# Layer normalisation without affine parts: an in-place ring of 8-row tiles, fixed engine orders and a short tail in place of six input and six output buffers of 4 rows

## The chip, the cores and the metric

The kernel runs on one core of one Trainium2 chip. The metric is the device time in microseconds (us) of a whole execution, the median of several; profiles give the span of one of them, which is about 2 us less. The kernel before takes 321.2 us. A run is called slow only when it is over 1.5% above the fastest of its kernel.

## The reference

```python
batch, seq, dim = 32, 512, 1024           # x: 16384 rows of 1024 float32, 67.1 MB
mean = np.mean(x, axis=-1, keepdims=True)
var = np.var(x, axis=-1, keepdims=True)
return ((x - mean) / np.sqrt(var + eps)).astype(np.float32)
```

Each row is read once and written once: 134.2 MB in all. Nothing can be left out.

## The kernel before

A tile is 4 rows a partition on 128 partitions, 2 MiB; a partition's 4 rows lie together in memory, so a DMA moves 128 pieces of 16 KiB, 8 on each of the 16 DMA engines. Loads are issued on the SyncE queue (q1 in the profile), stores on the ScalarE queue (q10).

```python
xin = ctx.enter_context(tc.tile_pool(name="xin", bufs=6))
yout = ctx.enter_context(tc.tile_pool(name="yout", bufs=6))
for t in range(ntiles):                                   # 32 tiles, K = 4
    xt = xin.tile([P, K, D], fdt)
    nc.sync.dma_start(out=xt, in_=x2[rows].rearrange("(p k) d -> p k d", p=P))
    ...      # VectorE: 2 bn_stats and 1 bn_aggr a row, then three tiny operations a tile
    ...      # ScalarE: square root; GpSimd: -mean * rstd
    yt = yout.tile([P, K, D], fdt)
    for k in range(K):
        nc.scalar.activation(out=yt[:, k, :], in_=xt[:, k, :], func=AF.Identity,
                             bias=nmr[:, k : k + 1], scale=rstd[:, k : k + 1])
    nc.scalar.dma_start(out=dst, in_=yt)
```

## Time and profile before

| | before |
|---|---|
| median time, us | 321.2 |
| span of the profiled run, us | 319.0 |
| busy: VectorE, ScalarE | 57%, 48% |
| DMA, mean of 16 engines | 98.8% of the span |
| rate between 40 and 280 us | 431 GB/s |
| last store's 16 landings: median, last | 315.69, 318.21 us |

The page is read from the DMA row: it is full from the second slice on, so engine times matter only where they empty a DMA queue. A DMA is complete when each of the 16 engines has reported; the trace holds those 16 reports. The difference between the last and the median one is called **lateness** below: 2.5 us before.

### The profile page before, as it was taken

To read this page: it belongs to the slowest core of one execution; us is meant where nothing else is said; L and a number is where in the kernel's file an instruction comes from. 1 tells how busy PE (TensorE), PEld (TensorE's weight loads), DVE (VectorE), ACT (ScalarE), POOL (GpSimd) and SP (SyncE) were. 2 spreads that over 40 slices of the span, in tenths; PEclk is the share of its full clock that TensorE was granted. 3 is DMA by queue.
4 is the path that set the end of the run, shared out by engine and by line. 5 is a ranking of instruction groups with operands and counts; after the bars stand their busy time and mean duration, and the time that the engine had idled before them with its cause. 6 is when DMAs were issued, how large, how long until landed. Compare 5 with 4: busy or idle time off the path is not lost.

```text
span 319.0 us, 926 instructions
## 1 busy us (share of the span) xinstructions
DVE 181.6 (57%) x480; ACT 154.3 (48%) x161; POOL 6.6 (2%) x36
## 2 busy tenths in 40 slices
DVE  0999764457754477544676355765446744467610
ACT  1147491651907419074380833809247091470970
POOL 0000000000000000000000000000000000000000
DMA  7999999999999999999999999999999999999995
GB/s 294 427 405 422 438 431 431 431 429 431 426 429 432 435 431 431 429 427 431 431 433 435 430 431 427 427 431 427 435 438 430 428 431 427 431 427 427 421 427 220
DMA packets 9222, 134.27 MB, mean 421 GB/s; under 512 B 1024, under 2 KB 1024, under 8 KB 1024
## 3 DMA queue, kind: packets, MB, share of 16 engines
q1 hardware_dynamic: 4608, 67.11, 49.6%
q10 hardware_dynamic: 4608, 67.11, 49.2%
q14 instruction: 6, 0.05, 0.0%
HBM read 67.11 MB, written 67.11 MB: 421 GB/s over the span
## 4 chain that ended last, share of the span: by engine, by line
DMA 87%; DVE 4%; issue 3%; ACT 2%; SPq 1%; POOLq 0%; POOL 0%; DVEq 0%
DMA xt<-in_x_dram 87%; DVE stats L53 3%; ACT yt L75 1%; SPq L47 1%; DVE mv L57 0%; DVE ivar L65 0%; DVE negmean L59 0%; POOLq L115 0%; ACT rstd L68 0%; POOL nmr L71 0%; DVE vpe L61 0%; DVEq L65 0%; DVEq L59 0%
## 5 line engine op out<-in xcount | busy, mean ns | idle before, releaser
L53 DVE BATCH_NORM_STATS2 stats<-xt 128x6 f32<-128x512 f32 x256 | 159.4, 665 | 115.3 <-DMA xt<-in_x_dram 115.3
L75 ACT ACTIVATE yt<-xt,nmr,rstd 128x1024 f32<-128x1024 f32 x128 | 146.7, 1227 | 4.7 <-POOL nmr L71 4.5
L68 ACT ACTIVATE rstd<-ivar 128x4 f32<-128x4 f32 x32 | 6.6, 205 | 149.6 <-DVE ivar L65 149.0
L57 DVE BATCH_NORM_AGGREGATE mv<-stats 128x2 f32<-128x12 f32 x128 | 25.1, 196 | 1.1
L71 POOL TENSOR_TENSOR nmr<-negmean,rstd 128x4 f32<-128x4 f32 x32 | 6.3, 198 | 297.9 <-ACT rstd L68 297.9
L65 DVE RECIPROCAL ivar<-vpe 128x4 f32<-128x4 f32 x32 | 5.7, 178 | 3.0
L59 DVE TENSOR_SCALAR negmean<-mv 128x4 f32<-128x4 f32 x32 | 5.4, 170 | 3.1
L61 DVE TENSOR_SCALAR vpe<-mv 128x4 f32<-128x4 f32 x32 | 5.2, 162 | 0.0
L68 ACT ACT_TABLE_LOAD x1 | 1.3, 1283 | 0.7 <-PEq L101 0.7
L101 POOL MEMSET const-float32-0.0<- 128x1 f32 x1 | 0.1, 98 | 0.2 <-issue 0.2
L101 POOL MEMSET const-uint8-127<- 128x1 uint8 x1 | 0.1, 102 | 0.0
L101 POOL MEMSET const-bfloat16-1.0<- 128x1 bf16 x1 | 0.1, 101 | 0.0
L101 POOL MEMSET const-float32-1.0<- 128x1 f32 x1 | 0.1, 98 | 0.0
## 6 DMA issues: line engine op xcount, KB each, us to landing
xt<-in_x_dram SPq DMA_DIRECT2D x32, 2048.0 KB, 38.4
out_dram<-yt ACTq DMA_DIRECT2D x32, 2048.0 KB, 15.5
```

The costliest lines, as they stand in the source:

```text
L47: nc.sync.dma_start(out=xt, in_=x2[rows].rearrange("(p k) d -> p k d", p=P))
L53: nc.vector.bn_stats(out=stats[:, k, s, :], in_=xt[:, k, s * BN_MAX : (s + 1) * BN_MAX],)
L57: nc.vector.bn_aggr(out=mv[:, k, :], in_=stats[:, k, :, :])
L59: nc.vector.tensor_scalar_mul(out=negmean, in0=mv[:, :, 0], scalar1=-1.0)
L61: nc.vector.tensor_scalar(out=vpe, in0=mv[:, :, 1], scalar1=eps_val, scalar2=None, op0=ALU.add)
L65: nc.vector.reciprocal(out=ivar, in_=vpe)
L68: nc.scalar.activation(out=rstd, in_=ivar, func=AF.Sqrt, bias=0.0, scale=1.0)
L71: nc.gpsimd.tensor_mul(out=nmr, in0=negmean, in1=rstd)
L75: nc.scalar.activation(out=yt[:, k, :], in_=xt[:, k, :], func=AF.Identity, bias=nmr[:, k : k + 1], scale=rstd[:, k : k + 1],)
L101: nc = _bacc.Bacc("TRN2", target_bir_lowering=False, num_devices=1)
```

## The change

The intent is to halve the number of packets (32 KiB instead of 16 KiB each), to write the result over the input so that all 192 KiB a partition serve both, to fix the order of instructions on each engine, to need fewer tiny operations, and to end on a small tile so that the last store is small and early. GROUP is the number of rows whose statistics are taken together; STORE is the number of rows after which a store is issued (16 is more than a tile, so there is one store a tile).

```diff
+TILES = (8, 8, 8, 8, 8, 8, 8, 8, 8, 8, 8, 8, 8, 8, 8, 6, 2)
+RING = 48
+GROUP = 4
+STORE = 16
-    xin = ctx.enter_context(tc.tile_pool(name="xin", bufs=6))
-    yout = ctx.enter_context(tc.tile_pool(name="yout", bufs=6))
+    ring = ring_pool.tile([P, RING, D], fdt)
...
-        nc.vector.tensor_scalar_mul(...)   # and add eps, reciprocal, ScalarE sqrt, GpSimd multiply
+        nc.scalar.activation(out=std[:, :G], in_=mv[:, :G, 1], func=AF.Sqrt, bias=eps_t, scale=1.0)
+        nc.vector.reciprocal(out=rstd[:, :G], in_=std[:, :G])
+        nc.vector.scalar_tensor_tensor(out=nmr[:, :G], in0=mv[:, :G, 0], scalar=-1.0,
+                                       in1=rstd[:, :G], op0=ALU.mult, op1=ALU.mult)
         for k in range(G):
             nc.scalar.activation(
-                out=yt[:, k, :],
+                out=xt[:, k, :],
...
+    with tc.manual_schedule():
+        nc.vector.memset(eps_t, eps_val)
+        for t, (K, row, pos) in enumerate(plan):
+            load(t)
+            ...                              # group(...) for every 4 rows, then store(...) for the tile
```

A load into a slot of the ring must now wait until the slot's store has landed.

More of the change, by code (lines that the diff above doesn't have):

```diff
@@ L26 @@
     BN_MAX = nc.vector.BN_STATS_FMAX
-    assert D % BN_MAX == 0
     NSUB = D // BN_MAX
-    K = 4
-    rows_per_tile = P * K
-    assert N % rows_per_tile == 0
-    ntiles = N // rows_per_tile
-    xin = ctx.enter_context(tc.tile_pool(name="xin", bufs=6))
-    yout = ctx.enter_context(tc.tile_pool(name="yout", bufs=6))
+    assert sum(TILES) * P == N
+    ring_pool = ctx.enter_context(tc.tile_pool(name="ring", bufs=1))
     st = ctx.enter_context(tc.tile_pool(name="st", bufs=4))
+    const = ctx.enter_context(tc.tile_pool(name="const", bufs=1))
     fdt = mybir.dt.float32
@@ L41, with load, group @@
     ALU = mybir.AluOpType
-    for t in range(ntiles):
-        rows = slice(t * rows_per_tile, (t + 1) * rows_per_tile)
-        xt = xin.tile([P, K, D], fdt)
-        nc.sync.dma_start(out=xt, in_=x2[rows].rearrange("(p k) d -> p k d", p=P))
-        stats = st.tile([P, K, NSUB, 6], fdt)
-        mv = st.tile([P, K, 2], fdt)
-        for k in range(K):
+    ring = ring_pool.tile([P, RING, D], fdt)
+    eps_t = const.tile([P, 1], fdt)
+    def load(t):
+        K, row, pos = plan[t]
+        rows = slice(row * P, (row + K) * P)
+        nc.sync.dma_start(
+            out=ring[:, pos : pos + K, :],
+            in_=x2[rows].rearrange("(p k) d -> p k d", p=P),
+        )
+    def group(xt, G):
+        stats = st.tile([P, GROUP, NSUB, 6], fdt, name="stats")
+        mv = st.tile([P, GROUP, 2], fdt, name="mv")
+        for k in range(G):
             for s in range(NSUB):
@@ L57 @@
             nc.vector.bn_aggr(out=mv[:, k, :], in_=stats[:, k, :, :])
-        negmean = st.tile([P, K], fdt)
-        nc.vector.tensor_scalar_mul(out=negmean, in0=mv[:, :, 0], scalar1=-1.0)
-        vpe = st.tile([P, K], fdt)
-        nc.vector.tensor_scalar(
-            out=vpe, in0=mv[:, :, 1], scalar1=eps_val, scalar2=None, op0=ALU.add
-        )
-        ivar = st.tile([P, K], fdt)
-        nc.vector.reciprocal(out=ivar, in_=vpe)
-        rstd = st.tile([P, K], fdt)
-        nc.scalar.activation(out=rstd, in_=ivar, func=AF.Sqrt, bias=0.0, scale=1.0)
-        nmr = st.tile([P, K], fdt)
-        nc.gpsimd.tensor_mul(out=nmr, in0=negmean, in1=rstd)
-        yt = yout.tile([P, K, D], fdt)
-        for k in range(K):
+        std = st.tile([P, GROUP], fdt, name="std")
+        nc.scalar.activation(
+            out=std[:, :G], in_=mv[:, :G, 1], func=AF.Sqrt, bias=eps_t, scale=1.0
+        )
+        rstd = st.tile([P, GROUP], fdt, name="rstd")
+        nc.vector.reciprocal(out=rstd[:, :G], in_=std[:, :G])
+        nmr = st.tile([P, GROUP], fdt, name="nmr")
+        nc.vector.scalar_tensor_tensor(
+            out=nmr[:, :G],
+            in0=mv[:, :G, 0],
+            scalar=-1.0,
+            in1=rstd[:, :G],
+            op0=ALU.mult,
+            op1=ALU.mult,
+        )
+        for k in range(G):
             nc.scalar.activation(
-                out=yt[:, k, :],
+                out=xt[:, k, :],
                 in_=xt[:, k, :],
@@ L81, with store @@
             )
+    def store(t, o, n):
+        K, row, pos = plan[t]
+        rows = slice(row * P, (row + K) * P)
         dst = o2[rows].rearrange("(p k) d -> p k d", p=P)
-        nc.scalar.dma_start(out=dst, in_=yt)
+        nc.scalar.dma_start(
+            out=dst[:, o : o + n, :], in_=ring[:, pos + o : pos + o + n, :]
+        )
+    plan = []
+    row = pos = 0
+    for K in TILES:
+        if pos + K > RING:
+            pos = 0
+        plan.append((K, row, pos))
+        row += K
+        pos += K
+    with tc.manual_schedule():
+        nc.vector.memset(eps_t, eps_val)
+        for t, (K, row, pos) in enumerate(plan):
+            load(t)
+            sent = 0
+            for g in range(0, K, GROUP):
+                G = min(GROUP, K - g)
+                group(ring[:, pos + g : pos + g + G, :], G)
+                if g + G - sent >= STORE or g + G == K:
+                    store(t, sent, g + G - sent)
+                    sent = g + G
 _INS = ['x', 'eps']
```

## The prediction

> **What bounds the kernel now.** I read the page from its top: first the busy shares, then the 40 slices, the DMA queues, the chain, the waits, and last the windows around the end.
>
> ```profile
> span 319.0 us, 926 instructions
> DVE 181.6 (57%) x480; ACT 154.3 (48%) x161; POOL 6.6 (2%) x36
> DMA  7999999999999999999999999999999999999995
> GB/s 294 427 405 422 438 431 431 431 429 431 426 429 432 435 431 431 429 427 431 431 433 435 430 431 427 427 431 427 435 438 430 428 431 427 431 427 427 421 427 220
> DMA packets 9222, 134.27 MB, mean 421 GB/s; under 512 B 1024, under 2 KB 1024, under 8 KB 1024
> q1 hardware_dynamic: 4608, 67.11, 49.6%
> q10 hardware_dynamic: 4608, 67.11, 49.2%
> ```
>
> No compute engine is at 60%, while the DMA digit is 9 from the second slice to the last but one. Loads (q1) and stores (q10) fill 98.8% of the time of 16 DMA engines. All bytes are compulsory: x in once, the result out once. So the kernel is bound by the DMA engines, and the chain and the waits only say so in other words:
>
> ```profile
> DMA 87%; DVE 4%; issue 3%; ACT 2%; SPq 1%; POOLq 0%; POOL 0%; DVEq 0%
> ...
> DVE stats L53 <- DMA xt<-in_x_dram: 115.3, 29, 8.6
> ```
>
> VectorE idles 115.3 us because its input has not landed, not the other way round. The middle of the run in the windows view:
>
> ```profile
> 40.00:280.00 240.00, 137.64 (x362) 119.02 (x124) 4.76 (x24) 1.00 1.01 431
> ```
>
> At 431 GB/s, 134.2 MB need 311.4 us. The span is 319.0, so 7.6 us are not steady transfer. I take them apart with the packet records of the trace. Before the first packet: 1.74 us. Ramp of the first 4 us: 143 GB/s where 431 from 1.9 us on would give 226, some 0.8 us. A dip where the first store joins (373 GB/s between 20 and 24 us): 0.5 us. After the last packet (317.88): 1.2 us. The rest is in the tail:
>
> ```profile
> 310.00:312.00 2.00, 0.00 (x0) 0.00 (x0) 0.00 (x0) 1.00 0.92 393
> 312.00:314.00 2.00, 0.00 (x0) 0.00 (x0) 0.00 (x0) 1.00 0.94 401
> 314.00:316.00 2.00, 0.00 (x0) 0.00 (x0) 0.00 (x0) 1.00 0.66 279
> 316.00:319.00 3.00, 0.00 (x0) 0.00 (x0) 0.00 (x0) 1.00 0.04 16
> ```
>
> The reader is to see the last line: 16 GB/s is not 16 engines slowed, it is a single one. In the packet records most of the final packets end by 315.40, and one chain goes on alone with ends at 315.45, 316.06, 316.67, 317.28 and 317.88, one packet every 0.61 us. One engine is thus 2.5 us late. The q14 records explain it: six 8192-byte packets fall inside the span (at 29.5, 83.3, 101.4, 179.5, 239.4 and 248.9 us), and at each one data packet took 851 to 1232 ns in place of 611. The six excesses sum to 533+240+611+342+240+621 = 2587 ns, just the lag. They come about every 127 VectorE instructions (four) and every 126 ScalarE instructions (two), so I read them as instruction fetches that all fall to one DMA engine. **The end is the chain of that engine**: 512 data packets, its ramp, and six fetches.
>
> **What the Trainium skill says.** (1) "DMA: Bandwidth & Descriptors", section "Where 436 GB/s comes from": 16 ports of 32 B at 850 MHz give 435.2 GB/s. Agrees as a ceiling: the best undisturbed second-by-second figures here are 431.5 to 432.1. (2) Same page, "Why small descriptors are slow (HBM only)": about 3 cycles of fixed overhead per packet. At 16 KiB the ceiling gives 16384/27.2 = 602.4 ns a packet; I measure a pitch of 606.8 ns (432.0 GB/s). Of the 4.4 ns, the 9 ns semaphore record that follows each engine's 8 packets of a DMA is 1.1; the other 3.3 ns are about 3 cycles at 850 MHz (3.5 ns). The trace agrees. (3) Same page, "Queues, rings and completion order": an engine goes round its queues packet by packet. The trace agrees: in the middle each 8 us hold about 105 load and 105 store packets. (4) "Runtime: NRT & Kernel Launch", "Instruction fetch mechanics", says refills are 16 KiB blocks of 256 instructions and mostly hidden; this trace shows 8192 bytes about every 127 instructions, and where the DMA engines are the bound they are not hidden. The measurement decides.
>
> **The change, part by part.**
> Bigger packets: 32 KiB in place of 16 KiB a partition. Bytes stay. By (2), a pair costs 2 x 602.4 + 3.3 + 1.1 = 1209.1 ns instead of 2 x 606.8 = 1213.6 (the semaphore record now follows 8 larger packets). That is 4.5 ns on 256 pairs an engine: **1.1 us saved**, all on the path. The steady rate should be about 433.6 GB/s.
> In-place ring: the buffers were six inputs and six outputs of 16 KiB a partition; now six of 32 KiB, the same 192 KiB. A load into a slot now waits for the landing of that slot's store, not for ScalarE's read. Does the load queue run dry? The first 4 MB load lands about 4.9 us later than the first 2 MB one did (8.6), 13.4 us. Two groups of statistics at about 5.9 us, two round trips of 0.3 and a last ScalarE group of 4.7 put the first store's issue at about 30 us (19.6 before). By then the queue still holds some 12 MB of the first 25 MB of loads, and at half the rate, 216 GB/s, it lasts past 85 us. The first store, sharing, needs 19.4 us and lands near 53, which frees the next load well before. In steady state a tile takes 19.4 us in and out, six of them 116 us; of that its own load and store use 39, compute 17, so about 60 us are spent queueing. Nothing runs dry: **0**.
> Fixed orders and the statistics: four tiny operations a group (multiply, add, reciprocal, GpSimd multiply) become a reciprocal and a scalar_tensor_tensor, on 33 groups rather than 32 tiles, so 64 VectorE instructions of 162 to 170 ns become 33. VectorE now waits for ScalarE's square root (about 0.3 us) in each group: 33 x 0.3 = 10 us. ScalarE's four normalisations take 4.65 us, under the 5.3 us of the next statistics, so the square root seldom waits. VectorE stays near 185 to 190 us of 318: **0** on the path.
> Tail of 6 and 2 rows: loads have a head start of about 32 us instead of 21, so they end near 283 us and over 13 MB of stores remain, 30 us. Statistics and normalisation of the last 2 rows take about 6 us and their store is issued near 296, some 15 us before the queue empties. Before, the last store was issued at 309.4 with its queue nearly empty: between 295 and 296 and between 300 and 301 only 13.0 and 13.8 of 16 engines were busy. That loss, (3.0+2.2)/16 = 0.3 us, goes, but the late engine, whose queue was behind, did not have it: **0 to 0.3**.
> Fetches: VectorE had 542 records, 59 of them semaphore waits, and would have 490 to 515. Its fourth fetch came at about 437, so it stays; ScalarE's second came near 192 and stays too. At best one goes, 0.4 us; I count 0.1.
> Sum: 1.1 + 0 to 0.3 + 0.1, so about 1.3 us off 321.2: **319.9**.
>
> **The rivals.**
> Rival A, the transfer gains nothing: the ports are the limit, the packets overlap (the records of the 16 engines sum to 16.1) and the overhead that I halve is hidden. For it: 8192-byte records take 309 ns and 16384-byte ones 611, almost exactly twice. Then 321.0.
> Rival B, a new wait: the load's wait for the store's landing, or the doubled first tile, drains a queue; or dependences on the one ring tile are taken more coarsely than by rows, and loads serialise with stores. The slack of 60 us speaks against the first; if it were so, DMA digits under 9 would show in the middle, and 5% idle would give 335.
> Rival C, the tail is the prize: with stores queued deeply, the whole of the 310-to-319 loss goes, 2.5 us, giving 317.5. Against it: one engine alone moves bytes there because of the fetches on it, and those remain.
> Rival D, larger strides between partitions (32 KiB) and between the engines' streams (256 KiB) meet in memory less well and lose 0.5%: 322.8. Nothing in the trace of before speaks for it.
>
> **Range and chances.** My account gives 319.9; A 321.0; C 317.5; D 322.8. The range 318.2 to 321.6 spans A and most of the way to C. Faster by 2% would need 314.8, which is below the 311.4 us of transfer at 431 GB/s plus the 1.74 before, the 1.2 after and the 2.2 us by which the timed run exceeds the span: nothing allows it except a rate near 435 and no straggler. Slower by 2% needs B. Faster 0.02, within 2% 0.95, slower 0.03.
>
> **What would show it right or wrong.** Right: half as many packets of data, 1219 to 1222 ns each; middle windows at 433 to 434 GB/s; first store near 30 us; last store issued 15 us or more before the end with the DMA digit at 9 to 315 us; one engine still alone in the last 2 to 3 us and five or six fetches on q14. Wrong: middle still 431 (A); digits under 9 in the middle or VectorE and the load queue waiting on stores (B); all engines ending together with six fetches (C); below 430 (D).

## The result

The changed kernel took 324.68 us in the median of 4 runs (323.44 to 325.87), the kernel before 321.29 on the same chip; the ratio of the fast runs is 1.0106 (95% interval 1.0079 to 1.0133), so within 2%, but slower. A ratio is the mean time of one kernel's fast runs over that of the other's of the same rounds, so it is not quite the ratio of the medians. On another chip it was 324.55 again (322.70 to 325.89). The spread is new: 2.4 and 3.2 us where all runs of the kernel before lie within 0.7.

The top of the page of the changed kernel, busy shares, slices and queues, in the profiled run (323.44 us, the fastest of the four):

```profile
span 321.7 us, 735 instructions
DVE 187.9 (58%) x451; ACT 159.4 (50%) x162; POOL 0.2 (0%) x4
...
DMA  8999999999999999999999999999999999999991
GB/s 326 448 403 452 388 432 416 456 407 440 441 412 440 436 413 448 424 424 440 424 424 452 416 432 452 404 444 440 416 436 424 416 437 429 431 440 417 430 418 69
DMA packets 4902, 134.27 MB, mean 417 GB/s; under 512 B 544, under 2 KB 544, under 8 KB 544
...
q1 hardware_dynamic: 2448, 67.11, 49.2%
q10 hardware_dynamic: 2448, 67.11, 48.4%
```

The data packets are halved, the bytes are the same, and the DMA row is still full. The rates of the slices scatter more than before, but what stands out is the last one: 69 GB/s, where before had 220. The windows view of the changed kernel (stretch, its length, busy time and count of VectorE, ScalarE and GpSimd, clock, DMA share, GB/s):

```profile
40.00:280.00 240.00, 149.63 (x357) 126.51 (x128) 0.00 (x0) 1.00 1.00 430
...
312.00:314.00 2.00, 0.00 (x0) 0.00 (x0) 0.00 (x0) 1.00 0.78 332
314.00:316.00 2.00, 0.00 (x0) 0.00 (x0) 0.00 (x0) 1.00 0.32 135
316.00:318.00 2.00, 0.00 (x0) 0.00 (x0) 0.00 (x0) 1.00 0.19 82
318.00:320.00 2.00, 0.00 (x0) 0.00 (x0) 0.00 (x0) 1.00 0.06 25
```

Before, the engines stopped together near 315.4 us and one went on alone. Now they stop one after another: ten by 314.1, others at 315.3, 315.9, 317.0, 317.7 and 317.7, and the last at 320.3. The reports of the last store say the same: median 314.37, last 320.75. **The middle engine finishes 1.3 us earlier than before, the last one is 6.4 us behind it instead of 2.5.** Together that is 2.5 us later (-1.3 + 3.9), nearly all of the 2.6 us by which the span grew.

The chain and the waits of the changed kernel:

```profile
DVE 45%; another core or an unknown queue 26%; DMA 16%; ACT 6%; issue 2%; SPq 0%; ACTq 0%
...
DVE stats L62 <- DMA ring<-in_x_dram: 80.7, 13, 12.2
DVE rstd L72 <- ACT std L68: 27.8, 33, 14.4
ACT std L68 <- DMA ring<-in_x_dram: 22.8, 1, 22.8
```

The chain now goes through VectorE, but VectorE still idles 80.7 us for loads, so it is not the bound. The 26% of "another core or an unknown queue" are such waits too (there is no other core here): one such piece starts at 183.34 us and lasts 6.65, and the timeline puts VectorE's idle time there down to a load (6.68 us before 190.02). The third wait shown is odd: ScalarE waits once, 22.8 us, for a load that it does not need. The timeline shows where (start, length, engine, and in brackets the idle time before):

```profile
202.86 4.63 ACT L83 ACTIVATE ring<-ring,nmr,rstd 128x1024 f32<-128x1024 f32 x4 [0.44 <-DVE nmr L74]
229.95 0.34 ACTq L95 DMA_DIRECT2D out_dram<-ring  x1
230.33 0.30 ACT L68 ACTIVATE std<-mv,eps_t 128x4 f32<-128x4 f32 x1 [22.84 <-DMA ring<-in_x_dram]
```

A finished tile lies from 207.5 to 229.95 us before its store is issued. The program's list of waits shows why: DMAs share eight completion semaphores, this store's semaphore had last been given to the load of tile 12, and that load landed at 229.87. This wait is new, and I suspected it first.

### The profile page after: what moved, and what is told of

The parts are those of the page before. It is cut to its first block, busy times and chain, and to the rows that moved or that the text cites. A ratio compares the mean times of both kernels' runs of the same rounds, so it can differ in the third digit from the quotient of the medians.

```text
span 321.7 us, 735 instructions
## 1 busy us (share of the span) xinstructions
DVE 187.9 (58%) x451; ACT 159.4 (50%) x162; POOL 0.2 (0%) x4
## 4 chain that ended last, share of the span: by engine, by line
DVE 45%; another core or an unknown queue 26%; DMA 16%; ACT 6%; issue 2%; SPq 0%; ACTq 0%
DVE stats L62 36%; DMA ring<-in_x_dram 16%; DVE mv L66 6%; ACT ring L83 4%; ACT std L68 3%; DVE rstd L72 2%; DVE nmr L74 1%; SPq L52 0%; ACTq L95 0%
## 5 line engine op out<-in xcount | busy, mean ns | idle before, releaser
L62 DVE BATCH_NORM_STATS2 stats<-ring 128x6 f32<-128x512 f32 x256 | 159.4, 664 | 80.7 <-DMA ring<-in_x_dram 80.7
L83 ACT ACTIVATE ring<-ring,nmr,rstd 128x1024 f32<-128x1024 f32 x128 | 148.4, 1229 | 14.6 <-DVE nmr L74 14.6
L68 ACT ACTIVATE std<-mv,eps_t 128x4 f32<-128x4 f32 (+1 forms) x33 | 9.8, 297 | 130.4 <-DVE mv L66 107.5
L66 DVE BATCH_NORM_AGGREGATE mv<-stats 128x2 f32<-128x12 f32 x128 | 26.7, 209 | 4.4
L72 DVE RECIPROCAL rstd<-std 128x4 f32<-128x4 f32 (+1 forms) x33 | 5.9, 178 | 27.8 <-ACT std L68 27.8
L74 DVE SCALAR_TENSOR_TENSOR nmr<-mv,rstd 128x4 f32<-128x4 f32 (+1 forms) x33 | 5.3, 162 | 1.1
```

The costliest lines, as they stand in the source:

```text
L62: nc.vector.bn_stats(out=stats[:, k, s, :], in_=xt[:, k, s * BN_MAX : (s + 1) * BN_MAX],)
L66: nc.vector.bn_aggr(out=mv[:, k, :], in_=stats[:, k, :, :])
L68: nc.scalar.activation(out=std[:, :G], in_=mv[:, :G, 1], func=AF.Sqrt, bias=eps_t, scale=1.0)
L72: nc.vector.reciprocal(out=rstd[:, :G], in_=std[:, :G])
L74: nc.vector.scalar_tensor_tensor(out=nmr[:, :G], in0=mv[:, :G, 0], scalar=-1.0, in1=rstd[:, :G], op0=ALU.mult, op1=ALU.mult,)
L83: nc.scalar.activation(out=xt[:, k, :], in_=xt[:, k, :], func=AF.Identity, bias=nmr[:, k : k + 1], scale=rstd[:, k : k + 1],)
```

## How the engines are counted

Three numbers are used below, all from the trace's packet records. **Slowed packets**: data packets that start after 45 us and take over 60 ns more than normal (606.5 ns for each 16 KiB). **Lateness**: last minus median report of the last store. **Distance**: the records do not name the engine, but on each engine a packet starts within a few ns of the end of the one before, so they can be linked into 16 chains; most chains then hold just the right number of packets (some swap a few). On each chain I counted, at every end of a store between 45 and 280 us, how many load packets had gone by since the end of a load. With 8 packets to a DMA in each queue and the queues taking turns, this distance mostly stays as it is set. The linking is not exact: a second linking of the same records gave the same main distance in every run, counts within some 10%, and losses after an end (given below) that are up to 24 ns higher.

| run | packet | time, median (range) | slowed packets, total excess | distance (cases) | lateness |
|---|---|---|---|---|---|
| before | 16 KiB | 321.2 | 5, 2.1 us | 2 (193), 3 (107) | 2.5 |
| changed | 32 | 324.7 (323.4-325.9) | 110, 21.6 | 1 (60), 2 (95) | 6.4 |
| e1_pad16 | 16 | 320.9 (320.8-321.1) | 5, 2.0 | 4 (155), 3 (36), of 16 | 3.2 |
| e2_k7 | 28 | 320.0 (319.9-320.2) | 11, 2.7 | 2 (209), 1 (14) | 3.2 |
| e3_ring40 | 32 | 323.0 (321.3-325.3) | 213, 65.1 | 1 (131), 2 (59) | 5.0 |
| e4_before_k8 | 32 | 324.7 (324.4-324.9) | 10, 2.3 | 0 (187) | 0.1 |
| e5_pad32 | 32 | 323.4 (320.2-325.6) | 47, 8.2 | 2 (111), 1 (40) | 5.0 |
| e6_k9 | 36 | 322.0 (321.6-322.1) | 42, 8.1 | 1 (170) | 4.5 |
| e11_k6 | 24 | 320.5 (320.3-320.6) | 5, 2.2 | 4 to 6 (226) | 1.9 |
| e12_k12 | 48 | 319.3 (318.9-323.7) | 15, 6.7 | 6 (100), 7 (27) | 3.0 |
| e13_delay4 | 32 | 320.1 (319.9-320.5) | 5, 2.3 | 5 (190) | 3.9 |
| e14_delay7h | 32 | 319.9 (319.7-322.5) | 23, 4.0 | 0 (181) | 3.3 |
| e15_after_again | 32 | 324.6 (322.7-325.9) | 225, 63.8 | 1 (129), 2 (28) | 3.8 |
| e16_delay8h | 32 | 324.2 (322.1-324.7) | 237, 49.5 | 1 (151), 2 (33) | 4.4 |
| e17_k12_shifted | 48 | 320.4 (320.1-321.3) | 15, 4.4 | 4 (93), 3 (32) | 3.9 |

The time is of all the runs of a version, the last three columns are of its one profiled run. Lateness alone misleads where nearly all engines lose time: in e15_after_again the median report of the last store came at 318.06 us, not 314.37, so its lateness of 3.8 is measured from a late middle.

## The experiments

Theories after the result: **P**, a long packet makes engines late by itself; **S**, the streams of the engines, a power of two apart in memory, collide; **W**, the semaphore wait at 207 us empties the store queue, and its new start makes engines late; and the ring itself. The edits below are shortened: constants stand where they are used.

**e1_pad16: 16 KiB packets in the same ring.**

```diff
-    ring = ring_pool.tile([P, RING, D], fdt)
+    ring = ring_pool.tile([P, RING // GROUP, GROUP * D + 8], fdt)   # 4 rows, then 32 bytes of padding
-TILES = (8, ..., 8, 6, 2)
+TILES = (8,) * 16
```

> The changed kernel with every tile's 8 rows cut into two pieces of 16 KiB by 32 bytes of padding in the buffer: same ring, same order, same walk through memory, but packets of 16 KiB (and a last tile of 8 rows instead of 6 and 2). Theory P (a long packet by itself makes some engines late): the last engine is at most 3 us behind the median one and the time is 320.5 to 321.8, steady rate back to 431. Theory S (the engines' streams, 256 KiB apart in memory, collide): the walk is the same, so the lag stays over 5 us and the time 323.5 to 325.5. Theory W (a store that waits for an unrelated load's semaphore, at about 208 to 230 us, drains the store queue, and its start again makes engines late): as S if the wait is still there.

320.87 us (ratio 0.9991, interval 0.9974 to 1.0008), 5 slowed packets, 431 GB/s between 40 and 280 us. The walk through memory is the same and the trouble is gone: S falls in the form in which I put it. The ring, the fixed order and the new statistics are cleared too, each as a cause by itself: they are all in this version. The tail of 6 and 2 rows is not; e13 below has it.

**e2_k7: 28 KiB packets.**

```diff
-TILES = (8, 8, 8, 8, 8, 8, 8, 8, 8, 8, 8, 8, 8, 8, 8, 6, 2)
-RING = 48
+TILES = (7,) * 18 + (2,)
+RING = 42
```

> The changed kernel with tiles of 7 rows (18 of them, then 2 rows; ring of 6 x 7 rows): packets of 28 KiB, streams of two neighbouring engines 224 KiB apart, no power of two. Theory P: nearly as the changed kernel, 323 to 325, last engine 5 us or more late. Theory S: lag of 3 us at most, 320 to 321.3. Theory W: follows whether ScalarE is held up for over 10 us once.

320.01 us (ratio 0.9962, interval 0.9947 to 0.9977), lateness 3.2 (theory S had asked for 3 at most), all four runs within 0.3 us. Theory P, by which 28 KiB should have been nearly as bad as 32, falls. This is the steadiest version that beats the kernel before.

**e3_ring40: five tiles instead of six.**

```diff
-RING = 48
+RING = 40
```

> The changed kernel with a ring of five tiles instead of six: fewer DMAs in flight for the eight completion semaphores, so the store that waits 22 us for a load's semaphore should wait less. Theory W: 320 to 321.5. Theories P and S: 323.5 to 325.5 with the late engines as before.

322.97 us, but in two groups: 321.28 and 321.34, 324.59 and 325.27. The profile fell in the upper group and shows 213 slowed packets. Inconclusive for W, but it tells that the trouble comes and goes from run to run.

**e4_before_k8: the kernel before with 32 KiB packets.**

```diff
-    K = 4
+    K = 8
-    xin ... bufs=6 ... yout ... bufs=6
+    xin ... bufs=3 ... yout ... bufs=3
```

> The kernel before with tiles of 8 rows and three input and three output buffers: 32 KiB packets without ring, without fixed order and with stores that never hold back a load. Theories P and S: late engines here too, 323 to 325. Theory W, or any theory that blames the in-place ring: 320 to 321.5.

324.67 us, as P and S said, but for another reason. Windows view of this run:

```profile
31.00:34.00 3.00, 2.93 (x10) 2.38 (x3) 0.00 (x0) 1.00 0.01 3
...
297.00:302.00 5.00, 3.33 (x11) 1.08 (x2) 0.20 (x1) 1.00 0.28 118
```

With three input buffers both queues are empty near 31 to 34 us (3 GB/s) and again near 297 to 302; the engines are not late at all (0.1 us at the last store). So 32 KiB packets can run cleanly. Had I read only the time, this run would have confirmed a wrong theory.

**e5_pad32: the slots of the ring no longer a power of two apart.**

```diff
-    ring = ring_pool.tile([P, RING, D], fdt)
+    ring = ring_pool.tile([P, RING // 8, 8 * D + 8], fdt)     # 8 rows, then 32 bytes of padding
```

> The changed kernel with only 32 bytes of padding between the six 32 KiB slots of the ring: packets stay 32 KiB, memory walk and order stay, but two slots' addresses in a partition no longer differ by a multiple of 32 KiB. Count of slowed data packets (over 60 ns above normal, after 45 us): 5 in the kernel before, 110 in the changed one, 213 with ring 40, 5 with 16 KiB pieces, 11 with 7 rows. Theory B (the load's writes and the store's reads meet in the buffer because the slots are a power of two apart): count under 20, time 319.8 to 320.8. Theory M (they meet in the chip's main memory, or long packets in a ring do it in any case): count over 60, time 323 to 325.5.

320.21, 321.44, 325.29 and 325.56 us: two groups again. The profiled run is one of the fast two (321.44 us) and still has 47 slowed packets, where theory B asked for under 20 and theory M for over 60. Separating the addresses in the buffer does not remove the effect; more this run does not tell.

**e6_k9: 36 KiB packets.**

```diff
-TILES = (8, ..., 8, 6, 2)
-RING = 48
+TILES = (9,) * 14 + (2,)
+RING = 45
```

> The changed kernel with tiles of 9 rows in a ring of five: packets of 36 KiB, longer than 32, and no distance a power of two, in the buffer or in memory. Theory L (packets of 32 KiB or more): count of slowed packets over 60, last engine 5 us or more behind the median one, 323 to 326. Theory B or any theory of powers of two: under 20, last engine at most 3.5 us behind, 320 to 321.5.

321.99 us, 42 slowed packets, 8.1 us in total: between the two again. Neither "32 KiB or more" nor "powers of two" fits.

**e7_store16: a store every 4 rows.**

```diff
-STORE = 16
+STORE = 4
```

> The changed kernel with a store for every 4 rows: stores in packets of 16 KiB, loads still 32 KiB, the ring's addresses unchanged. If it takes a long load packet against a long store packet, the count of slowed packets falls under 20 and the time to 320 to 321.5; if the long load packets alone do it, the count stays over 60 and the time at 323 to 325.5.

328.75 us (ratio 1.0239, interval 1.0219 to 1.0259): slower than either expected. Turns are taken by packet, so with 32 KiB loads and 16 KiB stores the loads get about two thirds of the rate (63 to 70% of the bytes between 30 and 60 us) and run ahead; their median time from issue to landing is 20.7 us, not 56.0, so they wait for room in the ring instead. One engine ends 10.2 us late. That this is what costs the time is not shown. It changes too much at once to answer its question.

**e8_inplace_before: the kernel before written in place, 8 rows, six buffers, without the fixed order.**

```diff
-    K = 4
+    K = 8
-        yt = yout.tile([P, K, D], fdt)
-                out=yt[:, k, :],
+                out=xt[:, k, :],
```

> The kernel before with 8 rows a tile, written in place, six buffers: the ring of 32 KiB tiles without the fixed order, the new statistics and the tail. If ring and packet size are enough, slowed packets over 60 and 323 to 325.5; if fixed order or statistics play a part, under 20 and 320 to 321.5.

322.46, 327.94, 332.22 and 335.26 us. Three of the four are slow, the profiled one too, so nothing is concluded from its 150 slowed packets; the one fast run, 322.46, was in neither expected range. Inconclusive.

**e9_more_instructions: is the last engine late because it fetches instructions?**

```diff
+        if t < 28:
+            for _ in range(24):
+                nc.vector.memset(scratch, 0.0)
```

> The kernel before with 672 tiny memsets of one column added on VectorE (about 0.06 us each, 40 us of an engine that is 43% idle), nothing else. If the end of the run is the chain of one DMA engine that also fetches instructions (8192 bytes for 128 of them, about 0.42 us of lateness each), 5 more fetches make the last engine about 4.6 us late instead of 2.5 and the time 323.0 to 323.6. If the lateness has another cause, the time stays at 321.1 to 321.5.

325.67 us (ratio 1.0140, interval 1.0124 to 1.0155). Eleven fetches fell into the span instead of six, and the five more cost 4.5 us, 0.9 each, twice what I expected. The windows view of this run says where most of it went:

```profile
292.00:296.00 4.00, 3.61 (x8) 0.00 (x0) 0.00 (x0) 1.00 0.80 340
296.00:300.00 4.00, 2.08 (x8) 1.35 (x2) 0.20 (x1) 1.00 0.35 147
```

The median report of the last load but one came at 279.27 us, the late engine's at 292.36, and VectorE started on that tile at 292.39. That is 13.1 us of lateness in the load queue, where the kernel before has 5.1 (283.41 and 288.50). No store was issued between 284.1 and 298.4 us, and the other engines ran out of stores: 147 GB/s. The last store adds it up: its median report came 3.9 us later than before (319.55, not 315.69), while its lateness was 3.2 us and not the 4.6 that I had expected. So fetches do make one engine late, but most of the price is paid by the other engines, which stand idle for want of stores.

**e10_k7_split: leave one engine out of the last tile.**

```diff
+        for a, b in ((0, 120), (120, 128)) if K == 2 else ((0, P),):
-            nc.sync.dma_start(out=ring[:, pos : pos + K, :], ...)
+            nc.sync.dma_start(out=ring[a:b, pos : pos + K, :], in_=src[a:b])     # stores likewise
```

> The version with 7 rows a tile (320.0 us) with its last tile of 2 rows moved as 120 and 8 partitions in place of 128, which leaves one DMA engine out of the last 1 MB in and out. If the engine left out is the late one (3.2 us behind in that version), the time is 317.3 to 318.3; if it is another, 320 to 320.6.

321.18 us, 1.2 more than without it. One chain ended at 309.1 us, the engine left out; the late one still ended last, at 318.2. It is another engine, and it got more work.

**e11_k6 and e12_k12: shorter and longer packets.**

```diff
-TILES = (8, ..., 8, 6, 2)
+TILES = (6,) * 21 + (2,)          # e11_k6; e12_k12: (12,) * 10 + (6, 2); RING = 48 in both
```

> The changed kernel with tiles of 6 rows, ring of eight: packets of 24 KiB. Slowed data packets after 45 us so far: 5 at 16 KiB, 11 at 28, 47 to 213 at 32, 42 at 36. If the length of the packet decides, at most 11 here and 320 to 320.8. If the power of two decides, also few: this is the lower control, it tells whether anything between 16 and 28 KiB is better.

> The changed kernel with tiles of 12 rows in a ring of four (then 6 and 2): packets of 48 KiB, no power of two. If length decides, slowed packets take more in total than the 8 us of 36 KiB packets, more than 10 us, and the last engine is over 4.5 us late, 322 to 327. If the trouble is the power of two, under 6 us in total beside the fetches; time then 321 to 323 for the deeper tiles alone.

24 KiB: 320.54 us (ratio 0.9980, interval 0.9963 to 0.9996), 5 slowed packets, as expected. 48 KiB: 318.94, 319.29 and 319.31 us, and one run of 323.73 (ratio 0.9972, interval 0.9906 to 1.0037); the rate between 60 and 220 us, 434 GB/s, is as high as in any run here. The median lies below both expected ranges, and 6.7 us of slowed packets, fetches included, are under the 10 of one theory. Less trouble with 48 KiB than with 32: length does not decide.

At this point I listed the slowed packets by chain. They sit at the ends of DMAs: typically one of the two load packets after the completion record of a store, on an engine whose own load had ended one packet earlier. The count by distance gave **theory O**: with 32 KiB packets, time is lost where a store ends one load packet after a load. In the changed kernel the three packets after such an end lost 107 ns on average in 60 cases, after a distance of two 5 ns in 95 cases. The distance is set when the first store joins the loads, that is when its first packet moves, at 34.3 us, and here it falls between one and two packets. Which of the two an engine gets differs from run to run: 60 and 95 cases in this profile, 129 and 28 in that of e15. The next runs move that moment.

**e13_delay4: the first store four packets later.**

```diff
     def store(t, o, n):
+        if t == 0:
+            for w in (1024, 1024, 1024, 1024):
+                nc.scalar.activation(out=ring[:, 0, :w], in_=ring[:, 0, :w],
+                                     func=AF.Identity, bias=0.0, scale=1.0)
```

> The changed kernel with four more normalising-sized instructions (identity, row 0 onto itself) on ScalarE ahead of the first store alone, so that the first store joins about 4.7 us, or some 4 packets of 32 KiB, later; all else the same. Counted on the engines' own chains, a store of the changed kernel ends one load packet after the load before it on the engines that lose time (60 cases, 0.11 us each) and two after it on the others (95 cases, 0.005 us); with rings of 40 rows one packet in 131 cases. Theory O (with 32 KiB packets the two queues' ends one packet apart cost time, and the distance is set once, by when the first store joins): ends now 5 or 6 packets apart, under 20 slowed packets, last engine at most 3.5 us late, 319.6 to 320.6. If the distance means nothing: 323 to 325.5 and over 40 slowed packets.

**320.13 us** (ratio 0.9968, interval 0.9953 to 0.9983) where the changed kernel itself took 324.55 on the same chip: 4.4 us gained by useless work that moves the first store, once, from 30.5 to 34.8 us. Distance 5 in 190 of 192 cases, 5 slowed packets. Windows view of this run:

```profile
60.00:220.00 160.00, 94.30 (x226) 78.90 (x80) 0.00 (x0) 1.00 1.00 432
312.00:314.00 2.00, 0.00 (x0) 0.00 (x0) 0.00 (x0) 1.00 0.75 315
314.00:316.00 2.00, 0.00 (x0) 0.00 (x0) 0.00 (x0) 1.00 0.09 37
316.00:318.00 2.00, 0.00 (x0) 0.00 (x0) 0.00 (x0) 1.00 0.04 16
```

Thirteen engines stop by 313.9 us, two by 314.5, and one goes on to 317.4, the picture of before. The lateness of 3.9 us is a little over my 3.5. This run also answers W: its timeline has the same long wait.

```profile
196.93 4.63 ACT L85 ACTIVATE ring<-ring,nmr,rstd 128x1024 f32<-128x1024 f32 x4 [0.44 <-DVE nmr L76]
223.83 0.34 ACTq L103 DMA_DIRECT2D out_dram<-ring  x1
224.22 0.30 ACT L70 ACTIVATE std<-mv,eps_t 128x4 f32<-128x4 f32 x1 [22.66 <-DMA ring<-in_x_dram]
```

ScalarE is held up 22.7 us here too, and the time is 320.1. Nor does the wait empty the store queue in the changed kernel itself, as W supposed; its windows view of the whole wait:

```profile
207.50:229.90 22.40, 5.57 (x12) 0.00 (x0) 0.00 (x0) 1.00 1.00 432
```

W falls.

**e14_delay7h: seven and a half instructions.**

```diff
+            for w in (1024,) * 7 + (512,):
```

> The same with seven and a half such instructions, about 8.8 us or 7.3 packets of delay: the distance comes round to 0 or 1 packet. Theory O: as many slowed packets as in the changed kernel or more (over 60), 322.5 to 326, although the store joins later than in the run with four. A theory that a later store helps by itself: 319.6 to 320.6.

319.73, 319.90, 319.95 and one run of 322.49 us. The distance in the profiled run came out at 0 (181 of 192 cases), not 1, and 0 was clean, as in e4_before_k8. The expected slowness did not come: the outcome is that of the rival, by which a later store helps by itself. But neither did the distance of one come, so this run did not test theory O, and e16 must decide between the two. The run of 322.49 us was not profiled; its distance is not known.

**e15_after_again: the changed kernel beside them**, without an edit.

> The changed kernel again, on the same chip as these two, to compare with: 323 to 326, over 60 slowed packets, as they were.

324.55 us. In this profile 129 of 192 cases have a distance of one, with 237 ns lost after each, and nearly every engine loses time. The windows view, the kernel before first and then this run:

```profile
60.00:220.00 160.00, 91.38 (x241) 79.41 (x84) 3.17 (x16) 1.00 1.01 431
...
60.00:220.00 160.00, 91.93 (x219) 77.03 (x78) 0.00 (x0) 1.00 1.00 426
```

**e16_delay8h: one instruction more than e14.**

```diff
+            for w in (1024,) * 8 + (512,):
```

> The changed kernel with eight and a half identity instructions ahead of the first store, one more than the run whose queues ended at the same packet on 181 of 192 occasions (319.9 us). One instruction is about one packet, so most engines should now have a store end one load packet after a load. Theory O: over 60 slowed packets, 322 to 326. If it stays under 25 slowed packets with the distance at one packet, theory O is wrong and it was the early part of the run that mattered.

**324.17 us** (ratio 1.0082, interval 1.0054 to 1.0110): distance 1 in 151 cases, 237 slowed packets. Windows view of this run:

```profile
60.00:220.00 160.00, 99.00 (x236) 83.44 (x84) 0.00 (x0) 1.00 1.01 429
...
314.00:316.00 2.00, 0.00 (x0) 0.00 (x0) 0.00 (x0) 1.00 0.75 320
316.00:318.00 2.00, 0.00 (x0) 0.00 (x0) 0.00 (x0) 1.00 0.33 139
```

One instruction, once, at 38 us, moves the end of the run by 4 us. First stores issued at 30.5, 34.8, 38.5 and 39.6 us gave 324.6, 320.1, 319.9 and 324.2: it is not "later is better", it goes round with the packets. The profiled runs with 32 KiB packets in the ring agree: with next to no ends at a distance of one (e13, e14) they took 320.5 and 319.9 us, with 40, 60, 129, 131 and 151 (e5, the changed kernel, e15, e3, e16) 321.4, 323.4, 324.5, 325.3 and 323.7. Theory O stands for 32 KiB packets, with one profile a version.

One rival is not tested by an edit: moving the first store also changes which addresses the two queues work on at the same time. Against it, the loss is not spread over a DMA: between two load ends an engine moves 16 data packets, and in e16 223 of 236 slowed packets are among the first seven of them, in e3 200 of 211, in e15 188 of 221 (in the changed kernel 76 of 108).

**e17_k12_shifted: 48 KiB packets with the ends four apart.**

```diff
+TILES = (8,) + (12,) * 9 + (8, 4)
+SLOT = 12                         # every tile takes a slot of 12 rows
```

> Packets of 48 KiB (319.3 us median, one run of four at 323.7; there the queues' ends were 6 or 7 packets of 8 apart, the 7 next to meeting) with a first tile of 8 rows, which lets the first store join after about 20 load packets: ends 4 apart, as far as they can be. Tail of 8 and 4 rows. Theory O: no slow run among six, under 15 slowed packets, 318.7 to 319.6. Otherwise a slow run of 322 or more among the six.

320.09 to 321.27 us over five runs, median 320.42 (ratio 0.9988, interval 0.9974 to 1.0002), 15 slowed packets, where I had asked for under 15. No slow run among the five, as hoped, but the time is 1.1 us above the good runs of e12_k12, out of my range, and I have not traced why: it has another first tile and another tail as well. It is no improvement on 7 rows a tile.

**What stays open**: why the distance of one costs so much at 32 KiB and little or nothing at other lengths. After such an end the loss was 70 to 271 ns on average with 32 KiB (changed kernel, e3, e5, e15, e16), 16 ns with 36 KiB (170 cases), and none with 28 KiB (14 cases) or 16 KiB (22 cases, kernel before). In the runs where most engines stand at one, the packets after a distance of two are slow as well (158 to 307 ns in e3, e15, e16), as if engines hindered each other. The Trainium skill, "DMA: Bandwidth & Descriptors", section "Queues, rings and completion order", says that an engine's semaphore write lands only after every earlier write of that engine, in all its queues; two such writes one long packet apart could hold each other up. No run here shows that this is the mechanism.

## Why the prediction was right or wrong

- **The bound** was right. The DMA row is full in both kernels, and e13 is 4.4 us faster although ScalarE does more work in it.
- **Bigger packets, 1.1 us saved on all engines**, was right in mechanism and nearly in size: undisturbed microseconds of the changed kernel run at 433.7 GB/s (predicted 433.6, before 432.0), and the middle engine ends 1.3 us earlier. Rival A, that nothing is gained, falls, though by the sign for it, a middle of 431, it would stand: the middle of the changed kernel shows 430, because slowed packets eat the gain. Where few packets are slowed, e2 and e13, the stretch from 60 to 220 us runs at 433 and 432. The record of a 32 KiB packet lasts 1213 ns at the median, not 1219 to 1222.
- **"The end is the chain of that engine: 512 data packets, its ramp, and six fetches" is the step that failed.** The sum took every other packet at its normal length. The chain did have six fetches (excess 2.5 us), and it does end alone, as predicted. But in the changed kernel other packets on it, and on five more engines that end late, took longer: 21.6 us of slowed packets instead of 2.1 after 45 us. The lateness grew from 2.5 to 6.4 us, and in the other profiled run of it nearly all engines were slowed. A term of 3.9 us is missing from the sum, against gains of 1.3. What brings it on is the distance of one packet between the queues' ends (e13 and e16), which I did not think of; why that costs time stays open. Nothing in the profile of before shows it: it has few cases of it, and there they cost nothing.
- **In-place ring: 0** was right in the time and wrong in a detail. The first store was issued at 30.5 us (30 predicted), the slack was there. It landed at 54.8; the "near 53" is about right, but the 19.4 us added to 30 give 49, so the sum shown does not lead to it. And "nothing runs dry" missed the semaphore wait of 22.4 us on ScalarE. e13 has the same wait at 320.1 us, and in the changed kernel the DMA share is 1.00 throughout it, so it is off the path. Rival B in its plain form falls.
- **Fixed orders and statistics: 0** was right: VectorE 187.9 us busy (185 to 190 predicted). Its waits for the square root were 27.8 us rather than 10, of which 14.4 is the one semaphore wait; all off the path.
- **Tail of 6 and 2 rows** was right in what it gains and wrong in its times. The last store was issued at 305.1 us, not near 296, because the last load landed at 299.0 (its median report came at 288.5, and 283 was predicted). That was still 16.6 us before the end of the span, more than the 15 predicted only because the end came later. It gains little because the tail is set by late engines.
- **Fetches**: six again, as counted. That they make one engine late is confirmed by e9. The price of 0.4 us each that I took into e9 was too low for that kernel (0.9 measured), since lateness of its loads also empties the other engines' queues.
- **Rival C**, that the whole loss at the tail goes, was wrong: it grew.
- **Rival D**, streams meeting in memory, was the nearest in size (322.8), but by luck: e1 walks through memory in the same way and is clean.
- **Range**: 318.2 to 321.6 was built from terms that the trace of before shows. It holds the medians of the changed kernel with the store delayed (320.1 and 319.9) and of e2_k7 (320.0), where the missing term is absent. It gave no room for engines drifting apart, though lateness was already the last 2.5 us of the kernel before.

## What to carry to other kernels

When a kernel is bound by DMA, look at the 16 reports of a DMA and not only at its landing: the time is that of the last engine, and a full DMA row does not show engines drifting apart. A change in packet size or buffering also changes where the ends of loads and stores fall against each other; if times become unsteady from run to run, move the first store by a few packets, or choose another number of rows, before judging the idea. And read why an experiment is slow before counting it for a theory: e4 had the expected time for an unrelated reason.

## What the Trainium skill lacked or had wrong

- "DMA: Bandwidth & Descriptors" has no word on the position of load ends against store ends. With 32 KiB packets a distance of 5 or 0 packets gave 320.1 and 319.9 us, a distance of 1 gave 324.2 and 324.6.
- Same page, "Rules for kernel authors": 128 partitions and at least 1 MiB per DMA are recommended for bandwidth, and that section has nothing against any size above it. Here a ring of six tiles took 320.0 us with 28 KiB a partition and 324.6 with 32 KiB, and a ring of four 319.3 with 48 KiB.
- Same page, "Why small descriptors are slow (HBM only)": the fixed cost of about 3 cycles per packet is worked out there for 256 bytes alone. The undisturbed rates here, 432.0 GB/s with 16 KiB and 433.7 with 32 KiB, differ by about what the same cost gives for large packets (433.6, the prediction's estimate from that page).
- "Runtime: NRT & Kernel Launch", "Instruction fetch mechanics": refills are given as 16 KiB and mostly hidden. Here they are 8192 bytes for about 127 instructions, and five more of them cost 4.5 us (e9).
- No page says that the issue of a DMA can be held up by the landing of an unrelated one because a program's DMAs share completion semaphores: ScalarE stood 22.4 us here, while the DMA share stayed at 1.00.
